# Weights, and the opening's conditioning columns, stored tile by tile in the chip's memory

## The chip, the cores and the metric

The kernel runs on one core of a Trainium2 chip. A core has a matrix engine (TensorE, PE in the profile), a vector engine (VectorE, DVE), a scalar engine (ScalarE, ACT), a general engine (GpSimd, POOL), an engine that here only issues transfers (SyncE, SP), and 16 DMA engines that move data between the memory outside the core (DRAM) and the core's 128-partition scratch memory. The metric is the device time of one execution in microseconds (us). Before the change the median of three runs is 2210.38 us (2209.37 to 2212.17).

## What is computed

A two-layer decoder trunk on 256 tokens of width 2048, all in float32. Layer 0 mixes tokens with a forgetting attention (FoX), layer 1 with a sliding-window attention (SWA); each is followed by a gated feed-forward block with a short convolution. Every sub-layer is shifted, scaled and gated by columns that come from one conditioning vector `c`:

```python
c_act = jax.nn.silu(c)
for i in range(DEPTH):
    mod = c_act @ ada_w[i] + ada_b[i]                    # 2048 x 12288 weights per layer
    sh1, sc1, g1, sh2, sc2, g2 = jnp.split(mod[:, None, :], 6, axis=-1)
    h = x * (1.0 + sc1) + sh1
    y = fox_attention(h, ...) if i % 2 == 0 else swa_attention(h, ...)
    x = layer_norm(ALPHA * x + (1.0 + g1) * y, ...)
    h = x * (1.0 + sc2) + sh2
    y = conv_ffn(h, ...)
    x = layer_norm(ALPHA * x + (1.0 + g2) * y, ...)
```

The weights are most of what is moved: `fox_w_in` 2048 x 6160, `fox_w_o` 2048 x 2048, `swa_w_in` 2048 x 2560, `swa_w_o` 2048 x 2048, and per layer `ffn_w_up` 2048 x 11264, `ffn_w_down` 5632 x 2048 and `ada_w` 2048 x 12288. `ffn` weights and `ada_w` exist once for each layer.

## The kernel before

**The weight stream.** Every matrix product goes through `stream`. It brings a weight tile `w` of 128 partitions x 2 x 512 float32 (512 KB): 256 rows of the weight and 512 of its columns. Partition p holds row p of the first 128 rows and row p of the second 128 rows, so it is filled by two pieces of 2 KB. ACT rounds the tile to the matrix engine's fast format (`wh`, L273), DVE forms the remainder (`wl`, L284), and PE multiplies three times (high by high, high by low, low by high). In `w_mm` the weights are stationary and the 256 tokens stream (banks `ws`, 24 matmuls for a tile), in `x_mm` the tokens are stationary and 512 weight columns stream (banks `xs`, 12 matmuls for a tile).

**The buffers and queues.** The pool `wp` has ten buffers of 512 KB that the tiles `w`, `wo`, `wa`, `wf` and `ln` share. All transfers of weights are issued by SP, in program order; a transfer waits until its buffer is free, and everything behind it waits too. The Tile framework's scheduler sets the order of the instructions on each engine, except where `pin` keeps program order.

**The opening.** Before the first product of layer 0 can be made, the columns `sh1` and `sc1` must be known: 2048 x 4096 numbers of `ada_w`. `opening` makes them in five steps. The first two steps make 256 of the 2048 columns of each of `sh1` and `sc1` (CB = 256), the last three make 512 (CB = 512). A step's tile `wo` has 1024 numbers in each partition: at CB = 256 it holds two row blocks k and k+1, each filled by a transfer of its own (256 KB in pieces of 1 KB), at CB = 512 one row block (512 KB in pieces of 2 KB). DVE multiplies each row block by one column of the activated vector `cact` and adds it into `oacc` (L605 for the first, L607 for the rest); in the first step four of the 16 row blocks go to PE instead. At the end of a step PE sums `oacc` over the partitions by matmuls with a column of ones (`cps`), DVE adds the bias (`cv`, L646), and the step's slice of the input is turned and modulated into `hH` and `hL`. The first products of FoX with those slices (`first_block`) are woven in between, so that weight tiles and `wo` tiles alternate in SP's queue.

**The rest.** The conditioning vectors of the later sub-layers are made in the background: tiles `wa` of `ada_w` (128 x 1024, one piece of 4 KB in each partition, L400) are woven into the weight stream and reduced by DVE (`acc`, L406). `forget` needs the 16 forget-gate columns of `fox_w_in`, which are brought by one transfer `wf` in 2048 pieces of 64 bytes (L825).

Of the kernel before, what the change touches and what calls it, by code (L numbers as in the profile page):

```python
# [17 lines left out]
P = 128  # L18
D = 2048
S = 256  # L20
NT = S // P
KC = D // P
DEPTH = 2
FH = 16
FW = 2048
# [11 lines left out]
WB = 512  # L37
# [4 lines left out]
def hybrid_trunk(ctx: ExitStack, tc: tile.TileContext, a: dict, out: bass.AP):  # L42
    nc = tc.nc
# [12 lines left out]
    def wtile(name="w"):  # L56
        return wp.tile([P, 2, WB], F32, tag="w", name=name)
# [7 lines left out]
    def bank(name="sm"):  # L65
        return psp.tile([P, 512], F32, tag="ps", name=name)
# [7 lines left out]
    def mm(o, lhsT, rhs, start=False, stop=False, **kw):  # L74
        return nc.tensor.matmul(o, lhsT, rhs, start=start, stop=stop, **kw)  # L75

    def pin(ins, on=True):

        if on:
            tc.keep_in_program_order(ins)  # L80
# [38 lines left out]
    x = cst.tile([P, NT, D], F32, name="x")  # L119
# [146 lines left out]
    def stream(wsrc, row0, col, ks, use, spare={}):  # L266

        for kc in ks[::2]:
            r0 = (row0 + kc) * P
            w = wtile()  # L270
            pin(nc.sync.dma_start(w, wsrc[r0:r0 + 2 * P, col:col + WB].rearrange("(k p) f -> p k f", p=P)), False)
            h, l = spare.get(kc) or (hl.tile([P, 2, WB], F32R, tag=n, name=n) for n in ("wh", "wl"))
            pin(nc.scalar.copy(h, w), False)  # L273

            def go(kc=kc, h=h, l=l):
                ahead[0] -= 1
                run_post()
                use(kc, h, l)
                if feeds:
                    feeds.pop(0)()  # L280
                tick()

            def residual_(w=w, h=h, l=l, go=go):
                pin(nc.vector.tensor_tensor(l, w, f32(h), op=ALU.subtract), behind[0] > 0)  # L284
                behind[0] -= 1
                del residuals[go]

            ahead[0] += 1
            weights.add(go)
            residuals[go] = residual_  # L290
            work.append(go)
            settle(2)
# [75 lines left out]
    def tick():  # L368
        ada_tick()
        if not feeds:  # L370
            step()
# [194 lines left out]
    def opening(plan, proj, prep):  # L566


        widths = [1, 1, 2, 2, 2]
        for v in range(2):  # L570
            cols[0, v] = cst.tile([P, KC], F32, tag=f"cv{v}", name="cv")


        onpe = [range(1, KC, 4), ()] + [(KC - 1,)] * 3

        def products(w, c0, CB, kc, ps, first):
            nb = CB // P
            for c in range(2 * nb):
                mm(ps[:, c:c + 1], w[:, c // nb, c % nb * P:(c % nb + 1) * P], cact[:, kc:kc + 1],
                   start=c == 0 and first, stop=kc == KC - 1, skip_group_check=True)  # L580

        def totals(CB, acc, ps, first, last):
            nb = CB // P
            for c in range(2 * nb):
                mm(ps[:, c:c + 1], acc[:, c // nb, c % nb * P:(c % nb + 1) * P], ones[:, 0:1],
                   start=c == 0 and first, stop=last, skip_group_check=True)

        def sums(s_, c0, CB, acc, ps):
            QK = 512 // CB
            pe = onpe[s_]  # L590
            for kq in range(0, KC, QK):
                w = wp.tile([P, QK, 2, CB], F32, tag="w", name="wo")
                for k in range(QK):
                    nc.sync.dma_start(w[:, k], a["ada_w"][0, (kq + k) * P:(kq + k + 1) * P, :2 * D]
                                      .rearrange("p (v f) -> p v f", f=D)[:, :, c0:c0 + CB])
                for k in range(QK):
                    kc = kq + k
                    end = kc == KC - 1
                    if kc in pe:
                        if end:  # L600
                            totals(CB, acc, ps, kc == pe[0], False)
                        products(w[:, k], c0, CB, kc, ps, kc == pe[0] and not end)
                        continue
                    if kc == 0:
                        nc.vector.tensor_scalar_mul(acc, w[:, k], cact[:, kc:kc + 1])  # L605
                    else:
                        nc.vector.scalar_tensor_tensor(acc, w[:, k], cact[:, kc:kc + 1], acc,  # L607
                                                       op0=ALU.mult, op1=ALU.add)
                    if end:
                        totals(CB, acc, ps, not pe, True)  # L610
                yield

        accs = cst.tile([P, D], F32, tag="acc", name="oacc").rearrange("p (c v f) -> p c v f", c=2, v=2)
        pair = 0
        todos = [[(*it, part) for it in items for part in range(3)] for items in plan]
        for s_, todo in enumerate(todos):
            n = len(todo)
            if s_ == len(widths):
                then(lambda: ada.update(rate=1.6))
                for it in todo:  # L620
                    proj(*it)
                break
            CB = widths[s_] * 2 * P
            nb, k0, c0 = CB // P, 2 * pair, pair * 2 * P
            pair += widths[s_]
            acc = accs[:, s_ % 2, :, :CB]
            ps = bank("cps")
            steps = [sums(s_, c0, CB, acc, ps)] * (KC * CB // 512)
            for i, g in enumerate(steps):
                if i == len(steps) // 2:  # L630
                    c = slice(c0, c0 + CB)
                    nc.sync.dma_start(x[:, :, c], a["x"][0][:, c].rearrange("(t p) d -> p t d", p=P))
                if s_ == 1:
                    while todo and n - len(todo) < -(-(i + 1) * n // len(steps)):
                        proj(*todo.pop(0))
                next(g)
                while todo and n - len(todo) < (i + 1) * n // len(steps):
                    proj(*todo.pop(0))

            for _ in range((1, 2, 2, 2, 2)[s_]):  # L640
                proj(*todos[s_ + 1].pop(0))
            for k in range(k0, k0 + nb, 2):
                tps = mod_turn(k, 2 if k == 0 else 1)
                if k == k0:
                    for v in range(2):
                        nc.vector.scalar_tensor_tensor(cols[0, v][:, k:k + nb], ps[:, nb * v:nb * (v + 1)], float(v),  # L646
                                                       acol[:, 0, v * KC + k:v * KC + k + nb],
                                                       op0=ALU.add, op1=ALU.add)
# [159 lines left out]
    def fox(l, j):  # L808
        w_in, w_o = a["fox_w_in"][j], a["fox_w_o"][j]
# [10 lines left out]
        def prep():  # L820
            for b in range(4):
                nc.sync.dma_start(bfc[32 * b:32 * b + FH, :], a["fox_b_f"][j:j + 1].rearrange("l h -> h l"))

            wf = wp.tile([P, KC, FH], F32, tag="w", name="wf")
            nc.sync.dma_start(wf, w_in[:, 3 * FW:3 * FW + FH].rearrange("(k p) f -> p k f", p=P))  # L825
            for q in range(4):
                src = wf[:, q * 4:(q + 1) * 4, :].rearrange("p k (o f) -> p k o f", o=1).broadcast_to([P, 4, 4, FH])
                th, tl = (i[q].rearrange("p k (b f) -> p k b f", b=4)[:, :, :, :FH] for i in (fh, fl))
                split(th, tl, src)
# [144 lines left out]
        for blk, rate in zip((0, 2, 1, 3), (1.6, 1.6, 1.5, 1.4)):  # L974
            then(lambda rate=rate: ada.update(rate=rate))
            q, k, V = [], [], []
            n = done.get((blk, 0), 0)
# [8 lines left out]
            o = old.get(blk, [None] * 3)  # L986
# [219 lines left out]
    for t in range(NT):  # L1206
        mu, rs, _ = moments[t]
        for d in range(D // 512):
            c = slice(d * 512, (d + 1) * 512)
# [2 lines left out]
            nc.sync.dma_start(ov[:, t, c], x[:, t, c])  # L1212


_INS = ["x", "c", "positions", "fox_w_in", "fox_b_f", "fox_w_o", "swa_w_in", "swa_sinks", "swa_w_o",
        "ada_w", "ada_b", "ffn_w_up", "ffn_conv_w", "ffn_conv_b", "ffn_w_down",
        "ln_mix_g", "ln_mix_b", "ln_ffn_g", "ln_ffn_b"]


# [19 lines left out]
```

## Time and profile before

| what | value |
|---|---|
| median of three runs | 2210.38 us (2209.37 to 2212.17) |
| span of the profiled execution, first to last instruction | 2210.7 us |
| PE busy | 2161.9 us (98%) |
| DVE busy | 1811.1 us (82%) |
| ACT busy | 1138.6 us (52%) |
| DMA: moved, mean rate | 602.98 MB, 273 GB/s |
| DMA packets | 274246, of which 243,592 of 2 KB up to 8 KB |

The profiled execution has no other time of its own than its span, which lies inside the range of the three runs. Busy time is the union of an engine's instructions. A matmul's end is modelled, so a PE that is busy throughout can still run below its best pace: the number of matmuls in a stretch tells that, and so does the granted clock (PEclk). "DMA share" is the mean busy share of the 16 DMA engines; it can exceed 1 a little, because the packets of an engine overlap. Times within the execution are counted from the span's start.

### The profile page before, as it was taken

What the parts mean: (1) busy time and instruction counts of PE and PEld (TensorE: products, weight loads), DVE (VectorE), ACT (ScalarE), POOL (GpSimd) and SP (SyncE); (2) the same over time, 40 slices, a digit from 0 to 9 for tenths busy, and PEclk for the clock granted to TensorE, in tenths of its full rate; (3) what the DMA queues carried; (4) which work ended last, traced back from release to release, by engine and by line L of the source; (5) the groups of instructions that cost most, each with busy time, mean ns of one, the idle gap of its engine ahead of it and who ended that gap; (6) DMA issues with size and microseconds to landing.
All of it is one profiled execution on the core that took longest, in us unless ns stands there. A gap on an engine that the chain in (4) does not pass through costs nothing.

```text
span 2210.7 us, 38191 instructions
## 1 busy us (share of the span) xinstructions
PE 2161.9 (98%) x14883; PEld 1973.9 (89%) x14883; DVE 1811.1 (82%) x2487; ACT 1138.6 (52%) x1713; POOL 19.9 (1%) x49
## 2 busy tenths in 40 slices
PE   6999999999999999999999999999999999999997
PEld 5999888789999988999987877789999988999986
DVE  6879998989978989889989888899888655666765
ACT  3435656465555533555534587545555533555541
POOL 0000000000000000000000000000000000000000
PEclk9999999999999999999999999999999999999999
DMA  9999998979978989889988666778888566666663
GB/s 341 367 343 373 347 357 297 329 256 325 344 238 297 323 299 365 287 266 325 311 281 312 229 200 201 258 269 293 281 270 267 188 194 193 195 195 192 195 198 112
DMA packets 274246, 602.98 MB, mean 273 GB/s; under 512 B 21062, under 2 KB 29960, under 8 KB 273552
## 3 DMA queue, kind: packets, MB, share of 16 engines
q1 hardware_dynamic: 273008, 595.85, 80.0%
q0 software_dynamic: 1056, 4.69, 0.6%
q8 instruction: 116, 1.90, 0.4%
q14 instruction: 66, 0.54, 0.1%
HBM read 598.37 MB, written 2.10 MB: 272 GB/s over the span
## 4 chain that ended last, share of the span: by engine, by line
PE 83%; DVE 9%; issue 3%; DMA 2%; ACT 2%; SPq 0%; POOL 0%; DVEq 0%; ACTq 0%; POOLq 0%
PE ws L75 47%; PE xs L75 32%; DVE acc L406 3%; DVE wl L284 2%; DMA wo<-in_ada_w_dram 2%; ACT wh L273 1%; PE sm L527 1%; PE cps L75 1%; PE S L75 1%; DVE pr L736 1%; PE o L75 0%; PE sm L75 0%; PE T L767 0%; DVE oacc L607 0%; DVE x L708 0%
## 5 line engine op out<-in xcount | busy, mean ns | idle before, releaser
L273 ACT CAST wh<-w 128x1024 fp32r<-128x1024 f32 x724 | 761.2, 1053 | 795.9 <-PE ws L75 297.9
L75 PE MATMUL ws<-hH,wh 128*128 128x256 f32 x6656 | 1150.6, 277 | 4.6 <-ACT hH L84 2.1
L284 DVE TENSOR_TENSOR wl<-w,wh 128x1024 fp32r<-128x1024 f32 x724 | 881.6, 1220 | 297.2 <-ACT wh L273 282.1
L75 PEld LDWEIGHTS ws<-hH,wh 128*128 128x128 f32 x6656 | 1011.0, 189 | 8.8 <-ACT hH L84 2.3
L75 PE MATMUL ws<-hH,wl 128*128 128x256 f32 x3328 | 918.3, 277 | 4.5 <-DVE wl L284 4.4
L75 PEld LDWEIGHTS ws<-hH,wl 128*128 128x128 f32 x3328 | 627.7, 189 | 6.3 <-DVE wl L284 6.1
L75 PE MATMUL xs<-wh,gT 128*128 128x512 f32 x1376 | 425.4, 389 | 0.0
L75 PEld LDWEIGHTS xs<-wh,gT 128*128 128x128 f32 x1376 | 258.3, 188 | 53.6
L75 PE MATMUL xs<-wl,gT 128*128 128x512 f32 x688 | 267.8, 389 | 0.0
L75 PE MATMUL xs<-wh,hH 128*128 128x512 f32 x704 | 235.9, 402 | 0.0
L406 DVE SCALAR_TENSOR_TENSOR acc<-wa,cact,acc 128x1024 f32<-128x1024 f32 x180 | 227.8, 1276 | 0.5 <-DMA wa<-in_ada_w_dram 0.5
L406 DVE SCALAR_TENSOR_TENSOR acc<-wa,cactp,acc 128x1024 f32<-128x1024 f32 x128 | 162.1, 1275 | 0.7 <-DMA acc<-in_ada_b_dram 0.7
L75 PEld LDWEIGHTS xs<-wh,hH 128*128 128x128 f32 x704 | 131.5, 189 | 28.9 <-ACT hH L84 0.3
L75 PEld LDWEIGHTS xs<-wl,gT 128*128 128x128 f32 x688 | 129.2, 188 | 26.5
L75 PE MATMUL xs<-wl,hH 128*128 128x512 f32 x352 | 139.4, 397 | 2.5 <-DVE wl L284 2.5
L1123 ACT ACTIVATE u<-ws,ccol 128x256 f32<-128x256 f32 x176 | 96.7, 561 | 62.2 <-PE ws L75 45.2
L75 PE MATMUL xs<-wh,oT 128*128 128x512 f32 x384 | 125.6, 396 | 0.0
L1124 DVE SCALAR_TENSOR_TENSOR u<-ws,ccol,u 128x255 f32<-128x255 f32 x176 | 82.3, 476 | 13.7 <-ACT u L1123 13.3
L75 PEld LDWEIGHTS xs<-wh,oT 128*128 128x128 f32 x384 | 72.1, 188 | 15.0
L1126 DVE SCALAR_TENSOR_TENSOR u<-ws,ccol,u 128x254 f32<-128x254 f32 x176 | 82.9, 476 | 2.0
L75 PEld LDWEIGHTS xs<-wl,hH 128*128 128x128 f32 x352 | 66.6, 189 | 17.7 <-DVE wl L284 4.3
L607 DVE SCALAR_TENSOR_TENSOR oacc<-wo,cact,oacc 128x1024 f32<-128x1024 f32 (+1 forms) x68 | 73.3, 1078 | 6.8 <-DMA wo<-in_ada_w_dram 5.7
(231 smaller groups left out, 1296.8 us busy)
## 6 DMA issues: line engine op xcount, KB each, us to landing
w<-in_ffn_w_up_dram SPq DMA_DIRECT2D x352, 512.0 KB, 4.7
wa<-in_ada_w_dram SPq DMA_DIRECT2D x320, 512.0 KB, 5.6
w<-in_ffn_w_down_dram SPq DMA_DIRECT2D x176, 512.0 KB, 5.0
w<-in_fox_w_in_dram SPq DMA_DIRECT2D x96, 512.0 KB, 7.3
wo<-in_ada_w_dram SPq DMA_DIRECT2D x48, 512.0 KB, 8.9
w<-in_swa_w_in_dram SPq DMA_DIRECT2D x40, 512.0 KB, 4.9
w<-in_fox_w_o_dram SPq DMA_DIRECT2D x32, 512.0 KB, 6.0
w<-in_swa_w_o_dram SPq DMA_DIRECT2D x32, 512.0 KB, 5.5
```

The costliest lines, as they stand in the source:

```text
L75: return nc.tensor.matmul(o, lhsT, rhs, start=start, stop=stop, **kw)
L273: pin(nc.scalar.copy(h, w), False)
L284: pin(nc.vector.tensor_tensor(l, w, f32(h), op=ALU.subtract), behind[0] > 0)
L406: pin(nc.vector.scalar_tensor_tensor(ac, wo, (cactp if row else cact)[:, k:k + 1], ac, op0=ALU.mult, op1=ALU.add), True)
L527: nc.tensor.transpose(o[:, t * P:(t + 1) * P], x[:, t, (k + j) * P:(k + j + 1) * P], ident)
L607: nc.vector.scalar_tensor_tensor(acc, w[:, k], cact[:, kc:kc + 1], acc, op0=ALU.mult, op1=ALU.add)
L736: nc.vector.tensor_tensor_reduce(pr[:, b:e].rearrange("p (a k) -> p a k", k=P), S_ps[:, b:e].rearrange("p (a k) -> p a k", k=P), mk, -1.0, ...
L1123: nc.scalar.activation(u, pf, AF.Identity, bias=cw(CW, f), scale=cw(2, f))
L1124: nc.vector.scalar_tensor_tensor(u[:, 1:], pf[:, :S - 1], cw(1, f), u[:, 1:], op0=ALU.mult, op1=ALU.add)
L1126: nc.vector.scalar_tensor_tensor(u[:, 2:], pf[:, :S - 2], cw(0, f), u[:, 2:], op0=ALU.mult, op1=ALU.add)
```

## The change

On the host, before the launch, the weights are stored in another order: for each tile the 2 KB pieces of a partition lie side by side, and the partitions of a tile follow each other, so that a tile is one run of 512 KB and each partition is filled by one run of 4 KB. This holds for all tiles of `stream`. The opening's slice of `ada_w` is stored once more (`ada_open`) in the same manner, so that a tile of CB = 256 comes in one transfer in place of two. The forget-gate columns become an array of their own (`fox_w_f`), one run of 1 KB for each partition. What lies in the scratch memory after a transfer is the same as before; no instruction of PE, DVE, ACT or POOL is added or removed.

```diff
     def stream(wsrc, row0, col, ks, use, spare={}):
         for kc in ks[::2]:
-            r0 = (row0 + kc) * P
             w = wtile()
-            pin(nc.sync.dma_start(w, wsrc[r0:r0 + 2 * P, col:col + WB].rearrange("(k p) f -> p k f", p=P)), False)
+            pin(nc.sync.dma_start(w, wsrc[(row0 + kc) // 2, col // WB]), False)
...
     def opening(plan, proj, prep):
-        widths = [1, 1, 2, 2, 2]
+        widths = list(STEPS)
...
                 w = wp.tile([P, QK, 2, CB], F32, tag="w", name="wo")
-                for k in range(QK):
-                    nc.sync.dma_start(w[:, k], a["ada_w"][0, (kq + k) * P:(kq + k + 1) * P, :2 * D]
-                                      .rearrange("p (v f) -> p v f", f=D)[:, :, c0:c0 + CB])
+                o = a["ada_open"][(c0 * KC + kq * CB) // 512]
+                nc.sync.dma_start(w.rearrange("p a b c -> p (a b c)"), o)
...
             wf = wp.tile([P, KC, FH], F32, tag="w", name="wf")
-            nc.sync.dma_start(wf, w_in[:, 3 * FW:3 * FW + FH].rearrange("(k p) f -> p k f", p=P))
+            nc.sync.dma_start(wf, a["fox_w_f"][j])
...
+STEPS = (1, 1, 2, 2, 2)
+
+def blocks(w):
+    l, k, n = w.shape
+    return w.reshape(l, k // (2 * P), 2, P, n // WB, WB).transpose(0, 1, 4, 3, 2, 5)
+
+def laid_out(a):
+    out = dict(a)
+    w = a["fox_w_in"]
+    out["fox_w_in"] = blocks(w[:, :, :3 * FW])
+    out["fox_w_f"] = w[:, :, 3 * FW:].reshape(-1, KC, P, FH).transpose(0, 2, 1, 3)
+    for n in ("fox_w_o", "swa_w_in", "swa_w_o", "ffn_w_up", "ffn_w_down"):
+        out[n] = blocks(a[n])
+    steps, c0 = [], 0
+    for s in STEPS:
+        cb = s * 2 * P
+        w = a["ada_w"][0, :, :2 * D].reshape(KC * cb // 512, 512 // cb, P, 2, D)[..., c0:c0 + cb]
+        steps.append(w.transpose(0, 2, 1, 3, 4).reshape(-1, P, 1024))
+        c0 += cb
+    out["ada_open"] = np.concatenate(steps)
+    return out
```

The scheduler is given transfers of another shape, so its order could have moved. SP's queue at the start of the program, before (`wo` are the opening's tiles, `w` the first FoX weights, `x` slices of the input):

```order
L96 DMA rows_76<-in_ada_b_dram 96x128
L594 DMA wo<-in_ada_w_dram 128x2x256 x8
L632 DMA x<-in_x_dram 128x2x256
L594 DMA wo<-in_ada_w_dram 128x2x256 x8
L271 DMA w<-in_fox_w_in_dram 128x2x512 x2
L594 DMA wo<-in_ada_w_dram 128x2x256 x2
L271 DMA w<-in_fox_w_in_dram 128x2x512
L594 DMA wo<-in_ada_w_dram 128x2x256 x4
```

And the same place with the change:

```order
L96 DMA rows_76<-in_ada_b_dram 96x128
L593 DMA wo<-in_ada_open_dram 128x1024 x4
L630 DMA x<-in_x_dram 128x2x256
L593 DMA wo<-in_ada_open_dram 128x1024 x4
L270 DMA w<-in_fox_w_in_dram 128x1024 x2
L593 DMA wo<-in_ada_open_dram 128x1024
L270 DMA w<-in_fox_w_in_dram 128x1024
L593 DMA wo<-in_ada_open_dram 128x1024 x2
```

Two transfers have become one in each tile of the first two steps, 16 fewer in all; the order of the tiles is the same, here and in the rest of SP's queue.

DVE at the end of the opening's second step, before (`wl` are remainders of FoX weights, `oacc` the products, `cv` the step's columns):

```order
L284 TENSOR_TENSOR wl<-w,wh 128x1024
L607 SCALAR_TENSOR_TENSOR oacc<-wo,cact,oacc 128x2x256 x4
L284 TENSOR_TENSOR wl<-w,wh 128x1024
L607 SCALAR_TENSOR_TENSOR oacc<-wo,cact,oacc 128x2x256 x3
L646 SCALAR_TENSOR_TENSOR cv<-cps,acol 128x2 x2
```

And with the change:

```order
L283 TENSOR_TENSOR wl<-w,wh 128x1024
L605 SCALAR_TENSOR_TENSOR oacc<-wo,cact,oacc 128x2x256 x4
L283 TENSOR_TENSOR wl<-w,wh 128x1024
L605 SCALAR_TENSOR_TENSOR oacc<-wo,cact,oacc 128x2x256 x4
L644 SCALAR_TENSOR_TENSOR cv<-cps,acol 128x2 x2
```

One product has moved behind the last remainder: the products of the last two tiles now stand together. Elsewhere on DVE three more instructions change places with a neighbour, on ACT two and on PE seven.

More of the change, by code (lines that the diff above doesn't have):

```diff
@@ L1212, in hybrid_trunk @@
             nc.sync.dma_start(ov[:, t, c], x[:, t, c])
-_INS = ["x", "c", "positions", "fox_w_in", "fox_b_f", "fox_w_o", "swa_w_in", "swa_sinks", "swa_w_o",
-        "ada_w", "ada_b", "ffn_w_up", "ffn_conv_w", "ffn_conv_b", "ffn_w_down",
-        "ln_mix_g", "ln_mix_b", "ln_ffn_g", "ln_ffn_b"]
+STEPS = (1, 1, 2, 2, 2)
[17 more added lines that the diff above has]
+    return out
 def kernel(**inputs):
@@ L1228 @@
     arrays, args = {}, {}
-    for name in _INS:
-        v = _np.ascontiguousarray(inputs[name])
+    for name, v in laid_out({n: _np.asarray(v) for n, v in inputs.items()}).items():
+        v = _np.ascontiguousarray(v)
         arrays[f"in_{name}_dram"] = v
```

## The prediction

> **What bounds the kernel now.** I read the page first, then the stretches of the span, then the chain of waits of the opening, then DVE in order of time, and last the rates of the transfers. From the page:
>
> ```profile
> span 2210.7 us, 38191 instructions
> PE 2161.9 (98%) x14883; PEld 1973.9 (89%) x14883; DVE 1811.1 (82%) x2487; ACT 1138.6 (52%) x1713; POOL 19.9 (1%) x49
> ...
> PE 83%; DVE 9%; issue 3%; DMA 2%; ACT 2%; SPq 0%; POOL 0%; DVEq 0%; ACTq 0%; POOLq 0%
> ...
> w<-in_ffn_w_up_dram SPq DMA_DIRECT2D x352, 512.0 KB, 4.7
> ```
>
> PE is busy for all but 48.8 us, and transfers hold 2% (some 44 us) of the chain that ended last. A change of transfers can win only from those. Where they lie, the stretches say (columns: stretch, length, busy time of PE, weight load, DVE, ACT, POOL with counts, granted clock, DMA share, GB/s):
>
> ```profile
> 0.00:10.00 10.00, 2.52 (x10) 2.14 (x10) 4.37 (x10) 5.75 (x10) 4.10 (x21) 1.00 0.66 199
> 10.00:20.00 10.00, 7.14 (x30) 6.49 (x31) 6.38 (x11) 0.00 (x0) 0.00 (x0) 1.00 1.08 366
> 20.00:30.00 10.00, 8.43 (x43) 8.05 (x44) 8.43 (x14) 5.45 (x7) 0.00 (x0) 1.00 1.08 366
> 30.00:40.00 10.00, 7.24 (x51) 6.46 (x49) 8.93 (x11) 4.65 (x8) 0.00 (x0) 1.00 1.08 364
> 40.00:50.00 10.00, 7.30 (x35) 7.24 (x36) 7.83 (x11) 2.09 (x2) 0.00 (x0) 0.66 1.04 385
> 60.00:150.00 90.00, 90.00 (x623) 84.80 (x622) 75.17 (x72) 36.66 (x45) 2.52 (x5) 0.92 1.01 360
> 150.00:300.00 150.00, 146.08 (x1115) 137.23 (x1114) 137.68 (x197) 87.33 (x168) 5.88 (x12) 1.00 1.01 357
> 500.00:750.00 250.00, 249.33 (x2161) 247.66 (x2161) 226.33 (x291) 138.86 (x190) 0.00 (x0) 1.00 0.89 303
> 1500.00:1750.00 250.00, 250.00 (x2161) 248.20 (x2161) 210.13 (x283) 141.84 (x195) 0.00 (x0) 1.00 0.81 266
> 1750.00:2100.00 350.00, 350.00 (x2506) 327.24 (x2505) 212.80 (x266) 170.06 (x210) 0.00 (x0) 1.00 0.65 194
> ```
>
> From 500 us on PE has no gap and the DMA engines have spare time: a faster transfer there buys nothing. DMA is full from 10 to 300 us, but from 60 to 150 PE is full too, and from 150 to 300 DVE is (137.68 of 150). Only the first 43 us are short of data. The chain there, in order of time (start, length, what):
>
> ```profile
> 11.24 5.89 DMA wo<-in_ada_w_dram
> ...
> 17.21 7.75 DMA wo<-in_ada_w_dram
> ...
> 32.09 7.74 DMA wo<-in_ada_w_dram
> ...
> 40.24 0.75 DVE oacc L607
> ...
> 42.70 1.84 PE cps L75 x8
> 44.54 5.09 PE ws L75 x24
> ...
> 143.14 9.47 DMA wo<-in_ada_w_dram
> ...
> 153.93 2.60 PE xs L75 x10
> ...
> 411.36 3.83 DMA wa<-in_ada_w_dram
> ...
> 417.13 4.74 DMA w<-in_fox_w_o_dram
> ```
>
> The opening's tiles pace it to 40 us, then the sums (`cps`) and PE. Later a transfer is on the chain three times. But the chain names one of two causes that end nearly together; DVE in the opening's second step (24.3 to 42.6 us) shows the other, first as groups of that stretch, then at the ends of steps one and two:
>
> ```profile
> L607 DVE SCALAR_TENSOR_TENSOR oacc<-wo,cact,oacc 128x512 f32<-128x512 f32 x15 | 11.3, 750 | 1.2 <-DMA wo<-in_ada_w_dram 0.9
> L284 DVE TENSOR_TENSOR wl<-w,wh 128x1024 fp32r<-128x1024 f32 x5 | 6.1, 1219 | 0.0
> ```
>
> ```profile
> 17.98 1.54 DVE L607 SCALAR_TENSOR_TENSOR oacc<-wo,cact,oacc 128x512 f32<-128x512 f32 x2 [0.68 <-DMA wo<-in_ada_w_dram]
> 21.48 0.23 DVE L646 SCALAR_TENSOR_TENSOR cv<-cps,acol 128x2 f32<-128x2 f32 x2 [1.96 <-PE cps L75]
> ...
> 38.43 0.75 DVE L607 SCALAR_TENSOR_TENSOR oacc<-wo,cact,oacc 128x512 f32<-128x512 f32 x1 [0.92 <-DMA wo<-in_ada_w_dram]
> ...
> 40.24 2.32 DVE L607 SCALAR_TENSOR_TENSOR oacc<-wo,cact,oacc 128x512 f32<-128x512 f32 x3
> ```
>
> In step two DVE waits for a transfer 0.92 us and is busy otherwise. So step one, to 19.5 us, is paced by transfers, and step two by DVE almost as much.
>
> **What a packet size is worth.** Three stretches, each of mostly one size, as moved at a full DMA: 10 to 16 us (1 KB), 44 to 60 (2 KB), 174 to 178 (4 KB: 1.65 MB in some 404 packets that are not small).
>
> ```profile
> DMA packets 2251, 2.17 MB, mean 362 GB/s; under 512 B 132, under 2 KB 2251, under 8 KB 2251
> ...
> DMA packets 3232, 6.23 MB, mean 390 GB/s; under 512 B 191, under 2 KB 191, under 8 KB 3231
> ...
> DMA packets 453, 1.65 MB, mean 413 GB/s; under 512 B 48, under 2 KB 48, under 8 KB 452
> ```
>
> So a byte in 4 KB pieces takes 362/413 = 0.877 of its time in 1 KB pieces, and 390/413 = 0.944 of that in 2 KB pieces. The Trainium skill ("DMA: Bandwidth & Descriptors", Why small descriptors are slow) gives a smaller loss: about 3 cycles for each packet beside one for 32 bytes. By that, 1 KB to 4 KB would save 6.4% (131 cycles against four times 35) and 2 KB to 4 KB 2.2%. The rows show 12.3% and 5.6%, about twice as much, and with the page's figures the sum below would end near -2.2 us; it goes by the rows.
>
> **The change part by part.** *Step one of the opening.* Its 16 row blocks are 16 x 256 KB = 4.19 MB: 11.6 us at 362 GB/s, 10.15 at 413, so -1.4. Against it stands the tile in one transfer: the last two row blocks now land together, and one product more (0.75 us) follows the last landing: +0.75. The start is the unknown. The first 10 us move only 199 GB/s. If that is the price of many small transfers, all 4.46 MB (with the slice of x) would land from 2.1 us on at 413, by 12.9, and step one end near 14.4 in place of 19.5: -5.1. If the start's slowness has another cause and the single transfer waits for its slowest DMA engine, nothing is left: 0. I take -1.2: the -0.65 from the rates and 0.5 for half as many transfers at the start, nearer to the rates since the rows with a full DMA carry them.
>
> *Step two.* Up to its last row block the DMA brings 4.19 MB of `wo` and six `w` (3.15 MB): -1.4 and -0.45, together with step one -3.2, less 0.75 for the coarser landing. But DVE has 17.4 us of products and remainders there that no transfer shortens; it can give back its 0.92 us at most. The smaller gain decides: -0.9, bounds 0 and -0.9. The one product that moves behind the last remainder costs nothing, since DVE works through both without a gap.
>
> *Steps three to five and the first FoX products.* The 48 tiles of 512 KB and the `w` go from 2 KB to 4 KB. PE is full from 60 to 150 us and the chain runs through PE from 42.7 to 130: 0. The `wo` transfer at 143 us (9.47 us) would take 5.6% less: -0.5, bounds 0 and -1.3.
>
> *`wf`.* Its 2048 pieces of 64 bytes hold up the DMA between 160 and 164 us:
>
> ```profile
> DMA packets 2481, 0.68 MB, mean 171 GB/s; under 512 B 2211, under 2 KB 2211, under 8 KB 2481
> ```
>
> Four us at 360 would have moved 1.44 MB, so about 2 us of DMA time are lost. PE has work queued (its idle time from 150 to 300 us is 3.9 in all), the tile itself is not needed until after 187 us. I take -0.3, bounds 0 and -1.6.
>
> *The rest.* The FoX output weight on the chain at 417 us: 5.6% of 4.74, taken as -0.2, bounds 0 and -1. FFN and SWA weights: 0; the work that hides them is PE's own, 250.00 of 250 us. Were PE 10% faster there, 303 GB/s of demand would come near the DMA's limit, and then 5.6% would count. SP issues 16 transfers fewer; it waits for buffers, not for itself.
>
> Sum: -1.2 - 0.9 - 0.5 - 0.3 - 0.2 = -3.1. Against the profile's own 2210.7 us that is 2207.6; the median of the runs lies 0.3 lower, so 2207.3.
>
> **Rivals.** *The transfers pace more than DVE and PE let me see.* From 60 to 150 us the DMA is at 1.01 of its time, and ACT waits for FoX weights there:
>
> ```profile
> ACT wh L273 <- DMA w<-in_fox_w_in_dram: 36.4, 17, 5.3
> ```
>
> If these waits reach PE, 107 us (43 to 150) shrink by 5.6%, -6.0, on top of -2.5 at 43 us: about 2202. Against it: PE is busy 90.00 of 90.
>
> *The clock.* From 40 to 50 us the granted clock is 0.66: nearly 7 us at half. PE then does 24 `ws` matmuls in 5.09 us. If shorter waits keep the clock up, 3.4 us more are won: 2203.9. It can as well lose the same elsewhere. The Trainium skill ("TensorE: Matmul & The Clock Gate", Part 1) says that the clock halves after an idle window of about 3.4 us, which runs free of the kernel; 0.66 over 10 us, two such windows at half, agrees, and by that rule a shift of the work alone can add or remove one.
>
> *Nothing comes of it.* The runs of 4 KB may go out as 2 KB packets, or the start stays as slow as it is and the coarser tiles take back the rest: 2209.5 to 2211.
>
> *Slower.* A tile in one run of 512 KB puts all 16 engines side by side in one part of the memory. If they hinder each other, the rate falls. The lowest for a busy engine here is 194/0.65 = 298 GB/s (1750 to 2100 us): the 12.06 MB to the end of step two (4.46 + 4.19 + 3.15 and a second slice of x) would take 7.4 us more than at 365, with the coarser landing some 8: 2218. It decides once the rate stays under 340 GB/s, the 303/0.89 of the feed-forward block. Against it: every row of `wa` already is 4 KB, and they go at 413.
>
> **How the numbers follow.** Forecast 0.43, own range 2205 to 2209.5; transfers pace more 0.24; clock 0.12; nothing 0.13; slower 0.08. The range of 2201.5 to 2211.5 holds the first four but for their tails. About 0.2% (4.4 us) is what a measurement of this kernel tells from no change. Faster than 2206: 0.24 + 0.12 and a little of the forecast, 0.38. Within: 0.40 of the forecast and 0.13, 0.53. Slower: 0.09.
>
> **What would show it.** Right: `wo` and `w` packets of 4 KB and over 400 GB/s from 10 to 40 us; the first `cv` near 20.3 us in place of 21.5; the first `ws` after the second step near 42.4 in place of 44.5, with DVE without a gap before it; stretches from 500 us on as before. Wrong: `cv` before 18 us (the start was a matter of transfers), a second step shorter by over 1 us (DVE was not its bound), PE from 60 to 150 us with more matmuls than 623 (the DMA paced it), or a full DMA under 390 GB/s.

## The result and the profile after

The change is faster by about 0.2%: 2204.98 us (median of 12 runs, 2203.63 to 2208.23) against 2209.86 us (12 runs, 2208.09 to 2212.57) of the kernel before, a ratio of 0.9978 with a 95% interval of 0.997 to 0.9986. The forecast was 2207.3, and 3.1 us gained; 4.9 were measured. Two later sets of runs of the same change gave 0.9982 (0.9973 to 0.9991) and 0.9982 (0.9974 to 0.9991), that is 3.5 and 4.1 us. The profiled executions stand 8.2 us apart, more than any of the medians; why is the main question below.

Here are lines of the page of the kernel after: span, busy times, DMA packets, and the shares of the chain that ended last.

```profile
span 2202.5 us, 38162 instructions
...
PE 2156.7 (98%) x14883; PEld 1968.9 (89%) x14883; DVE 1810.4 (82%) x2487; ACT 1139.3 (52%) x1713; POOL 19.9 (1%) x49
...
DMA packets 166598, 602.98 MB, mean 274 GB/s; under 512 B 18758, under 2 KB 19592, under 8 KB 165904
...
PE 84%; DVE 10%; issue 3%; ACT 2%; DMA 1%; SPq 0%; POOL 0%; DVEq 0%; ACTq 0%; POOLq 0%
```

The layout took effect: the same 602.98 MB go in 166,598 packets in place of 274,246, and the DMA's share of the chain is 1% in place of 2%. PE is idle for 45.8 us (48.8 before), and is busy 5.2 us less with the same 14,883 matmuls. So 3.0 of the 8.2 us are waits of PE that are gone, and 5.2 are PE's own pace, which the runs below trace to its clock and not to the transfers.

The stretches of the kernel after (columns as in the prediction: stretch, length, PE, weight load, DVE, ACT, POOL, granted clock, DMA share, GB/s):

```profile
10.00:20.00 10.00, 6.71 (x28) 6.06 (x28) 6.29 (x10) 1.04 (x1) 0.00 (x0) 1.00 1.02 408
20.00:30.00 10.00, 8.42 (x47) 8.12 (x47) 9.85 (x16) 6.34 (x9) 0.00 (x0) 1.00 1.03 411
30.00:40.00 10.00, 6.10 (x41) 5.33 (x39) 9.75 (x13) 4.96 (x7) 0.00 (x0) 0.91 1.03 406
40.00:50.00 10.00, 9.32 (x48) 8.49 (x48) 7.11 (x9) 1.46 (x3) 0.00 (x0) 0.75 1.03 410
...
60.00:150.00 90.00, 89.43 (x630) 83.28 (x629) 78.20 (x76) 35.92 (x43) 2.52 (x5) 0.96 0.98 373
...
500.00:750.00 250.00, 249.33 (x2132) 246.52 (x2132) 226.34 (x291) 139.24 (x191) 0.00 (x0) 1.00 0.87 305
...
1750.00:2100.00 350.00, 350.00 (x2505) 327.24 (x2504) 212.36 (x265) 169.78 (x209) 0.00 (x0) 1.00 0.62 194
```

From 10 to 50 us the DMA moves 406 to 411 GB/s where it moved 364 to 385. Behind 500 us its share falls by 0.02 to 0.03 at nearly the same GB/s: the same bytes cost less of its time, and nobody needs that time. From 1750 to 2100 us PE does 2505 matmuls, as it did 2506.

Rows of VectorE in order of time, after (start, duration, and in brackets the idle time ahead and what ended it):

```profile
20.04 0.23 DVE L644 SCALAR_TENSOR_TENSOR cv<-cps,acol 128x2 f32<-128x2 f32 x2 [1.96 <-PE cps L75]
...
42.26 0.23 DVE L644 SCALAR_TENSOR_TENSOR cv<-cps,acol 128x2 f32<-128x2 f32 x2 [2.02 <-PE cps L75]
```

The second `cv` of before:

```profile
44.58 0.23 DVE L646 SCALAR_TENSOR_TENSOR cv<-cps,acol 128x2 f32<-128x2 f32 x2 [2.02 <-PE cps L75]
```

And all that VectorE waited for from 20 to 45 us after the change (total, times, longest):

```profile
DVE cv L644 <- PE cps L75: 4.0, 2, 2.0
```

The first `cv` comes at 20.04 in place of 21.48, the second at 42.26 in place of 44.58. In the second step VectorE now waits for no transfer at all; before it waited 0.92 us for a `wo`. The chain of waits shows the same end of step two (start, length, what):

```profile
42.22 4.22 PE ws L75 x24
```

The first products start at 42.22 in place of 44.54. This is 2.3 us of lead. The medians show 4.9 and the profiles 8.2.

### The profile page after: what moved, and what is told of

Read it like the earlier page. It is cut to its first block, busy times and chain, and to the rows that moved or that the text cites. A ratio compares the mean times of both kernels' runs of the same rounds, so it can differ in the third digit from the quotient of the medians.

```text
span 2202.5 us, 38162 instructions
## 1 busy us (share of the span) xinstructions
PE 2156.7 (98%) x14883; PEld 1968.9 (89%) x14883; DVE 1810.4 (82%) x2487; ACT 1139.3 (52%) x1713; POOL 19.9 (1%) x49
## 2 busy tenths in 40 slices
DMA packets 166598, 602.98 MB, mean 274 GB/s; under 512 B 18758, under 2 KB 19592, under 8 KB 165904
## 4 chain that ended last, share of the span: by engine, by line
PE 84%; DVE 10%; issue 3%; ACT 2%; DMA 1%; SPq 0%; POOL 0%; DVEq 0%; ACTq 0%; POOLq 0%
PE ws L75 47%; PE xs L75 33%; DVE wl L283 3%; DVE acc L405 3%; DMA wo<-in_ada_open_dram 1%; ACT wh L272 1%; PE cps L75 1%; PE sm L526 1%; PE S L75 1%; DMA w<-in_fox_w_in_dram 1%; PE o L75 1%; DVE pr L734 1%; DVE oacc L605 0%; PE sm L75 0%; PE T L765 0%
## 5 line engine op out<-in xcount | busy, mean ns | idle before, releaser
L75 PE MATMUL xs<-wl,oT 128*128 128x512 f32 x192 | 75.4, 393 | 3.1 <-DVE wl L283 3.1
```

## The experiments

The theory under test was the one of the prediction: the opening's two steps give the gain, and weights in larger pieces give nothing, since PE or VectorE bound the rest. Its rivals were that transfers pace PE up to 150 us, and that the clock decides. Each run is stated against runs of the kernel before on the same chip. "Ratio" is the time over that of before, with its 95% interval in brackets. Code cuts are shortened; `...` marks what is left out.

**The opening alone.** All streamed weights and `wf` stay as before; only `ada_open` is laid out, one transfer for each tile.

```diff
-            nc.sync.dma_start(wf, a["fox_w_f"][j])
+            nc.sync.dma_start(wf, w_in[:, 3 * FW:3 * FW + FH].rearrange("(k p) f -> p k f", p=P))
...
-    out["fox_w_in"] = blocks(w[:, :, :3 * FW])
...
-    for n in ("fox_w_o", "swa_w_in", "swa_w_o", "ffn_w_up", "ffn_w_down"):
+    for n in ():
         out[n] = blocks(a[n])
```

> Only the opening's tiles are stored tile by tile and come in one transfer each; all other weights and the forget-gate columns lie and come as before. Theory (the gain is made in the first two steps of the opening, by their own tiles, and what is more than 2.3 us of it is the clock): the first columns near 20.1 us (before 21.5, with the whole change 20.0), the first matmuls after step two between 42.2 and 42.9 (44.5 and 42.2), and the time 2.5 to 5 us below before. Rival (the FoX weights pace PE from 43 to 150 us): less than 2 us below before, since these weights come as before.

Measured: 2204.94 us (2203.39 to 2211.09), ratio 0.9987 (0.9978 to 0.9997), profiled span 2202.6. VectorE's rows and one stretch of this kernel:

```profile
20.20 0.23 DVE L648 SCALAR_TENSOR_TENSOR cv<-cps,acol 128x2 f32<-128x2 f32 x2 [1.96 <-PE cps L75]
...
42.41 0.23 DVE L648 SCALAR_TENSOR_TENSOR cv<-cps,acol 128x2 f32<-128x2 f32 x2 [2.02 <-PE cps L75]
...
60.00:150.00 90.00, 89.43 (x630) 83.22 (x629) 78.21 (x76) 36.11 (x44) 2.52 (x5) 0.96 1.01 371
```

With the old weights, and the DMA full again (1.01 in place of 0.98), PE does the same 630 matmuls from 60 to 150 us as with the new ones, and its span is that of the whole change to 0.1 us. The transfers of weights don't pace PE there. The ratio is a little nearer to 1 than those of the whole change, with overlapping intervals. Its interval, 0.7 to 4.9 us of gain, would by itself allow the rival's less than 2; it is the count of matmuls that speaks against the rival.

**The streamed weights alone**, with the opening as before.

```diff
-                o = a["ada_open"][(c0 * KC + kq * CB) // 512]
-                nc.sync.dma_start(w.rearrange("p a b c -> p (a b c)"), o)
+                for k in range(QK):
+                    nc.sync.dma_start(w[:, k], a["ada_w"][0, (kq + k) * P:(kq + k + 1) * P, :2 * D]
+                                      .rearrange("p (v f) -> p v f", f=D)[:, :, c0:c0 + CB])
...
```

> Only the streamed weights and the forget-gate columns are stored tile by tile; the opening's tiles lie and come as before. Theory: the first columns at 21.5 us as before, the matmuls after step two at most 0.5 us earlier than 44.5, and the time within 1.5 us of before (PE and DVE hide these transfers). Rival (FoX weights pace): 3 us or more below before, won between 43 and 150 us.

Measured: 2207.86 us (2205.16 to 2211.89), ratio 0.9998 (0.9989 to 1.0006), profiled span 2205.5.

```profile
21.82 0.22 DVE L649 SCALAR_TENSOR_TENSOR cv<-cps,acol 128x2 f32<-128x2 f32 x2 [1.96 <-PE cps L75]
...
44.02 0.23 DVE L649 SCALAR_TENSOR_TENSOR cv<-cps,acol 128x2 f32<-128x2 f32 x2 [2.02 <-PE cps L75]
```

All 728 streamed tiles are laid out here, and nothing comes of it that can be measured; the interval leaves room for up to 2.4 us. The first step is as late as before. The second takes 22.20 us from `cv` to `cv`, the same as in the whole change (22.22): without a wait for a transfer this is VectorE's own work, and the 2.0 us that it waits for PE's sums.

**The late weights alone** (`fox_w_o`, SWA and FFN, 632 of 728 tiles). The edit is against the kernel before. Up to 336 us, when the first tile of `fox_w_o` is issued, this program issues the same instructions and the same transfers as that kernel.

```diff
+def laid_out(a):
+    out = dict(a)
...
+    for n in ('fox_w_o', 'swa_w_in', 'swa_w_o', 'ffn_w_up', 'ffn_w_down'):
+        out[n] = blocks(a[n])
+    return out
```

> Only the weights used after the FoX input projection (FoX output, SWA, both feed-forward blocks: 632 of 728 streamed tiles) are stored tile by tile; FoX input weights, forget-gate columns and the opening come as before. Theory: no change, within 0.7 us of before, since PE is full where these tiles come. Rival (faster landing reaches PE at the stage boundaries, or the tiles' one place in memory slows the transfers): 1.5 us or more off before, either way.

Measured: 2212.12 us (2206.49 to 2214.19), ratio 1.0007 (0.9997 to 1.0016): no gain, so the late weights give nothing that can be measured. The median lies 3.1 us above that of before, where 0.7 at most was expected; these runs had a lower granted clock, and the five of them at 0.992 take 2212.75 us in the mean, where before takes 2212.35 (table below). But the profiled execution spans 2206.3 us, 4.4 less than the profiled one of before. What VectorE waited for from 20 to 45 us in it, and the stretch from 50 to 150 us:

```profile
DVE oacc L610 <- DMA wo<-in_ada_w_dram: 0.3, 1, 0.3
...
50.00:150.00 100.00, 96.94 (x689) 88.96 (x689) 87.06 (x83) 41.66 (x51) 2.52 (x5) 0.98 1.05 386
```

The same stretch of the kernel before:

```profile
50.00:150.00 100.00, 97.89 (x661) 91.67 (x660) 81.63 (x79) 39.62 (x49) 2.52 (x5) 0.91 1.02 363
```

Two executions of the same instructions, with the same old layout: 689 matmuls at a granted clock of 0.98, 661 at 0.91. So one profile against one profile says nothing at the size of some microseconds here, unless the clocks agree. The wait of 0.92 us in step two is not fixed either: it is 0.3 here.

**The change once more**, for a second and a third profile.

> The whole change once more, with a second profile. Theory (2.3 us are won by data up to 42 us, the rest of the first comparison is where the half-clock stretches happen to fall): the first columns at 20.0 us and the matmuls after step two within 0.5 us of 42.2 as in the first profile, but half-clock stretches at other places or of other number; the time 2 to 5 us below before; runs with equal mean clock within about 1 us of each other. Rival (all 4.9 us are the transfers'): the same stretches in the same places, and the same lead at each point of the program as in the first profile.

> The whole change a third time, beside the next kernel on one chip. Theory (data to 42 us, then the clock): the first columns at 20.0 to 20.2 us, the second at 42.2 to 42.4, whatever the total; the time 2 to 5 us below before; runs of equal mean clock some 3 us below those of before. Rival: no lead at equal clock.

Measured: 2205.59 us (2202.45 to 2209.58) and 2204.78 us (2202.88 to 2208.23); profiled spans 2207.8 and 2203.8. The second profile is the useful one, since it had the clock of the profile of before. The cores view of before and of the second profile of the change:

```profile
core 0: 2210.7 us, clock 0.992
```

```profile
core 0: 2207.8 us, clock 0.992
```

Four stretches of before, and the same four, 3 us earlier, of the second profile (the granted clock is the third number from the end):

```profile
36.00:51.00 15.00, 9.53 (x50) 9.10 (x50) 11.26 (x14) 4.10 (x5) 0.00 (x0) 0.77 1.05 380
...
76.00:88.00 12.00, 12.00 (x74) 11.70 (x73) 6.30 (x9) 4.46 (x6) 0.00 (x0) 0.72 0.98 344
117.00:130.00 13.00, 13.00 (x79) 12.29 (x78) 5.46 (x9) 4.33 (x5) 0.00 (x0) 0.74 1.04 378
1205.00:1215.00 10.00, 8.17 (x29) 5.24 (x28) 8.81 (x21) 5.53 (x9) 1.54 (x2) 0.83 0.24 88
```

```profile
33.00:48.00 15.00, 9.83 (x57) 9.46 (x56) 12.69 (x17) 5.04 (x6) 0.00 (x0) 0.77 1.03 409
...
73.00:85.00 12.00, 12.00 (x75) 11.83 (x74) 6.26 (x9) 2.28 (x4) 0.00 (x0) 0.72 0.85 308
114.00:127.00 13.00, 13.00 (x80) 12.38 (x79) 5.79 (x9) 4.17 (x5) 0.00 (x0) 0.74 0.98 373
1202.00:1212.00 10.00, 8.16 (x30) 5.15 (x29) 8.81 (x21) 5.65 (x9) 1.54 (x2) 0.83 0.14 55
```

The clock pattern is the same, moved by about 3 us with the work. In the first profile of the change three of these stretches ran faster:

```profile
76.00:88.00 12.00, 12.00 (x80) 11.27 (x80) 9.96 (x13) 4.71 (x7) 0.00 (x0) 0.86 0.89 311
114.00:127.00 13.00, 13.00 (x90) 12.35 (x90) 7.89 (x12) 4.45 (x7) 0.00 (x0) 0.87 0.97 376
1202.00:1212.00 10.00, 9.55 (x47) 7.61 (x48) 10.00 (x19) 6.64 (x12) 0.00 (x0) 1.00 0.27 84
```

By these rows it kept (0.86 - 0.72) x 12 + (0.87 - 0.74) x 13 + (1.00 - 0.83) x 10 = 5.1 us of full clock more than the second profile, which is 5.3 us longer. So with equal clocks the two executions lie 2210.7 - 2207.8 = 2.9 us apart, and 5.3 of the 8.2 us between the first two profiles are the clock. The same instructions of before and of the second profile say where the 2.9 arise:

```profile
122.33 0.23 DVE L646 SCALAR_TENSOR_TENSOR cv<-cps,acol 128x4 f32<-128x4 f32 x2 [5.31 <-PE cps L75]
...
172.64 3.50 DVE L284 TENSOR_TENSOR wl<-w,wh 128x1024 fp32r<-128x1024 f32 x3 [0.20 <-ACT wh L273]
...
180.40 0.69 DVE L887 SCALAR_TENSOR_TENSOR ql<-ws,qh 128x512 fp32r<-128x512 f32 x1
...
206.18 0.22 DVE L189 CAST posf<-posr 2x128 f32<-2x128 int32 x1 [0.49 <-DMA posr<-in_positions_dram]
...
257.74 0.57 POOL L394 DMA_DIRECT2D acc<-in_ada_b_dram  x1 [48.72 <-PE sm L470]
...
1094.47 0.59 POOL L394 DMA_DIRECT2D acc<-in_ada_b_dram  x1 [620.36 <-DVE red L452]
```

```profile
20.07 0.23 DVE L644 SCALAR_TENSOR_TENSOR cv<-cps,acol 128x2 f32<-128x2 f32 x2 [1.96 <-PE cps L75]
...
42.29 0.23 DVE L644 SCALAR_TENSOR_TENSOR cv<-cps,acol 128x2 f32<-128x2 f32 x2 [2.02 <-PE cps L75]
...
119.73 0.23 DVE L644 SCALAR_TENSOR_TENSOR cv<-cps,acol 128x4 f32<-128x4 f32 x2 [5.39 <-PE cps L75]
...
169.67 3.50 DVE L283 TENSOR_TENSOR wl<-w,wh 128x1024 fp32r<-128x1024 f32 x3 [0.23 <-ACT wh L272]
...
177.74 0.69 DVE L885 SCALAR_TENSOR_TENSOR ql<-ws,qh 128x512 fp32r<-128x512 f32 x1 [0.92 <-ACT qh L884]
...
203.31 0.21 DVE L189 CAST posf<-posr 2x128 f32<-2x128 int32 x1 [0.27 <-DMA posr<-in_positions_dram]
...
254.87 0.57 POOL L393 DMA_DIRECT2D acc<-in_ada_b_dram  x1 [48.65 <-PE sm L469]
...
1091.59 0.59 POOL L393 DMA_DIRECT2D acc<-in_ada_b_dram  x1 [620.34 <-DVE red L451]
```

And two pieces of the second profile's chain of waits:

```profile
42.26 4.90 PE ws L75 x24
...
151.28 2.59 PE xs L75 x10
```

The lead of the second profile is 1.41 us at the first `cv`, 2.29 at the second, 2.60 at the third (122.33 against 119.73), 2.65 on PE at 154 (153.93, behind the `wo` at 143 us, against 151.28), 2.97 at 172, 2.66 again at 180, 2.87 at 257 and 2.88 at 1094. Step one and step two give 2.3 of the 2.9. The rest comes in small steps. From 44 to 55 us the 24 matmuls behind the sums take 4.90 us in place of 5.09, which is the half clock ending earlier beside the work (0.2). Then ScalarE no longer rounds a weight tile ahead of `hH`, as it did in its order before (0.2). At 206 us VectorE waits 0.27 us for the transfer of the positions where it waited 0.49 (0.2); in the first profile of the change this wait is 0.48, so it isn't the layout's. So 2.3 us are the layout, 0.2 more come of the moved order, and the rest is what differs from one execution to another. From 257 us on nothing is won.

Many runs show about the same. Here are the means of all runs of before and of the whole change that list their granted clock, grouped by it (four runs of before at 0.991, with a mean of 2213.44 us, have no counterpart):

| granted clock | before, us (runs) | the change, us (runs) | difference |
|---|---|---|---|
| 0.992 | 2212.35 (14) | 2209.58 (1) | -2.8 |
| 0.993 | 2209.56 (19) | 2207.71 (7) | -1.8 |
| 0.994 | 2208.83 (43) | 2205.19 (14) | -3.6 |
| 0.995 | 2207.18 (13) | 2203.81 (10) | -3.4 |
| 0.996 | 2205.70 (1) | 2202.66 (2) | -3.0 |

At equal clock the change wins about 3 us. Over all these runs the means differ by 4.2 (2209.43 in 94 runs, 2205.28 in 34), since the mean clock is higher with the change, 0.99415 against 0.99353: an estimated 0.00062 x 2207 = 1.4 us. Grouped in the same way, the opening alone is 3.2 us below before at 0.995 (6 runs) and 1.6 at 0.992 (3 runs); the streamed weights alone are 0.9 below at 0.994 (5 runs).

**Two transfers for a tile.** The whole change, but each tile of the first two steps comes in two transfers, one for each row block, in pieces of 2 KB.

```diff
-                o = a["ada_open"][(c0 * KC + kq * CB) // 512]
-                nc.sync.dma_start(w.rearrange("p a b c -> p (a b c)"), o)
+                o = a["ada_open"][(c0 * KC + kq * CB) // 512].rearrange("p (a b c) -> p a b c", a=QK, b=2)
+                for k in range(QK):
+                    nc.sync.dma_start(w[:, k], o[:, k])
```

> As the whole change, but a tile of the first two steps comes in two transfers again, one for each row block, in pieces of 2 KB (in place of one transfer in pieces of 4 KB, or before two in pieces of 1 KB). Theory (the piece size counts, and the coarser tile costs one product, 0.75 us, that the rates pay back): pieces of 2 KB at 390 GB/s against 1 KB at 362 give 0.85 us of the 1.4, the finer landing 0.75: the first columns between 19.7 and 20.5 us, the time within 1.5 us of the whole change. Rival (the number of transfers makes the start slow): the first columns at 21 us or later, the time 1.5 us or more above the whole change.

Measured: 2208.05 us (2204.08 to 2210.58), ratio 0.9991 (0.9981 to 1), span 2202.3; the first `cv` at 20.39, the second at 42.60. That is 0.3 us behind the whole change at both places, so the rival (21 us or later) is refuted. Two row blocks that can land one after the other in pieces of 2 KB are no better than both at once in pieces of 4 KB. The median lies 3.1 us above the first one of the whole change, where 1.5 at most was expected; the intervals of the ratios overlap, so the times don't separate the two.

**One transfer in pieces of 1 KB.** The whole change, but the tiles of the first two steps are stored so that their one transfer fills each partition by four runs of 1 KB.

```diff
-                nc.sync.dma_start(w.rearrange("p a b c -> p (a b c)"), o)
+                wv = w.rearrange("p a b c -> p (a b c)")
+                if CB == 256:
+                    o = o.rearrange("p f -> (p f)").rearrange("(q p f) -> p q f", q=4, p=P)
+                    wv = wv.rearrange("p (q f) -> p q f", q=4)
+                nc.sync.dma_start(wv, o)
...
+        if cb == 256:
+            t = t.reshape(-1, P, 4, 256).transpose(0, 2, 1, 3).reshape(-1, P, 1024)
```

> As the whole change, but the tiles of the first two steps, still one transfer each, are filled in four runs of 1 KB for each partition in place of one of 4 KB. Theory (the piece size is what counts): 1 KB pieces at 362 GB/s and the coarser landing, so the first columns between 21.5 and 22.3 us, not before the kernel before (21.5), the time 1 to 3 us above the whole change. Rival (half as many transfers is what counts): the first columns at 20 to 20.7 us as in the whole change.

Measured: 2205.94 us (2203.51 to 2209.14), ratio 0.9984 (0.9975 to 0.9993), span 2204.2.

```profile
21.11 0.23 DVE L652 SCALAR_TENSOR_TENSOR cv<-cps,acol 128x2 f32<-128x2 f32 x2 [1.96 <-PE cps L75]
```

The first `cv` stands between what the two theories gave. Against the whole change, whose first `cv` came at 20.04, 20.07 and 20.14, the size of the pieces alone is worth 1.0 us, by this one execution. Against the old opening, seen at 21.46 (late weights), 21.48 (before), 21.82 (streamed weights) and 22.37 (before with idle matmuls, below), three things that changed together are worth 0.35 to 1.3 us: half as many transfers, the coarser landing, and the place in memory, since the 1 KB pieces of a tile lie in one run here and in rows of `ada_w`, 48 KB apart, before. The run with two transfers has finer landing and smaller pieces as well, so it doesn't separate them, and the place in memory wasn't tested by itself.

**Two row blocks of step two on PE.** If VectorE bounds step two, products taken from it must shorten it.

```diff
-        onpe = [range(1, KC, 4), ()] + [(KC - 1,)] * 3
+        onpe = [range(1, KC, 4), (13, 14)] + [(KC - 1,)] * 3
```

> The whole change, and two of the sixteen row blocks of the opening's second step (the 14th and 15th) are multiplied and summed on PE in place of DVE. Theory (DVE bounds the second step): two products of 0.76 us leave DVE behind the last landing, the second columns come 1.2 to 1.5 us earlier than 42.3 us. Rival (transfers bound it): less than 0.4 us earlier, or later.

> The whole change with two row blocks of the second step on PE, a second time, beside the whole change on one chip. Theory (PE bounds everything behind 42 us, and the clock decides what of a lead lasts): the second columns again near 40 us, the time 0 to 2 us below the whole change. Rival (the lead of 2.2 us at 40 us lasts in full): 2 us or more below the whole change.

Measured in two sets: 2204.49 us (2200.86 to 2206.17), ratio 0.9978 (0.9969 to 0.9987), and 2204.18 us (2199.4 to 2207.32), ratio 0.9977 (0.9968 to 0.9986). The second `cv`, and PE's clock later, in the first of them:

```profile
40.03 0.23 DVE L648 SCALAR_TENSOR_TENSOR cv<-cps,acol 128x2 f32<-128x2 f32 x2 [1.28 <-PE cps L75]
...
113.00:125.00 12.00, 12.00 (x66) 11.21 (x67) 6.66 (x10) 2.39 (x5) 0.00 (x0) 0.72 0.90 345
```

VectorE does bound step two: the second `cv` comes 2.2 us earlier than in the change's first profile, and at 39.67 in the second of the two sets. 1.5 of the 2.2 are two products of 0.76; the other 0.7 is VectorE's wait for PE's sums, 1.28 us in place of 2.02, since these took 0.95 us at full clock in place of 1.83 at half. But the span is 2202.5, that of the change: at 113 to 125 us this execution has a clock of 0.72, where the change's first profile had 0.87 in nearly the same stretch. On PE the lead is still 2.3 us at 110 us, and 12 x 0.15 = 1.8 us of it are gone there. The intervals overlap those of the change (0.9973 to 0.9991), so a gain beyond it isn't shown.

**Holding the clock up.** Matmuls whose result isn't used (ten calls, which stand as twenty in the trace) are put in PE's gap ahead of the sums of step two, in the whole change and, apart from it, in the kernel before.

```diff
+                if s_ == 1 and i == len(steps) - 1:
+                    spin(bank("spin"), 10)
                 next(g)
```

> The whole change, and ten idle matmuls of 384 columns (their result is not used) in PE's gap ahead of the second step's sums, so that PE is not idle there. Theory (an idle PE brings the half clock behind it): the half-clock stretch at 38 to 45 us goes or halves, the matmuls behind the second step gain 1.7 to 3.4 us, and the time is 1 to 3.4 us below the whole change at most runs. Rival (the clock falls regardless of PE's own idle time): stretches as before, the time within 1 us of the whole change or above it.

> The kernel before, with the same ten idle matmuls in the same gap. Theory (clock): 1 to 3.4 us below before, with transfers as before. Rival: no change.

Measured: with the change 2206.14 us (2204.2 to 2206.88), ratio 0.9985 (0.9976 to 0.9993); in the kernel before 2208.84 us (2206.39 to 2210.74), ratio 0.9996 (0.9987 to 1.0005). The idle matmuls and the second `cv` of the first, and two stretches of it:

```profile
35.20 6.61 PE L75 MATMUL spin<-mask,ident 128*128 128x384 f32 x20
...
42.64 0.23 DVE L650 SCALAR_TENSOR_TENSOR cv<-cps,acol 128x2 f32<-128x2 f32 x2 [2.31 <-PE cps L75]
```

```profile
36.00:47.00 11.00, 11.00 (x59) 8.27 (x58) 8.55 (x12) 2.10 (x3) 0.00 (x0) 1.00 1.03 409
...
113.00:125.00 12.00, 12.00 (x67) 11.20 (x66) 5.57 (x9) 2.71 (x4) 0.00 (x0) 0.72 0.99 379
```

The low clock of the first stretch is gone (1.00), but at 113 to 125 us it is 0.72, and no time is won in either kernel. The theory's gain failed to appear in both. The run is not a clean test of it: the idle matmuls outlast the gap. VectorE's last product ends at 40.34 us, the sums start only at 41.81, and the second `cv` comes 0.4 us later than in the whole change (42.64); in the kernel before the sums start at 44.72, 1.0 us behind the last product. It shows one thing about the table above: with the idle matmuls the whole change has a mean clock of 0.9956 in its eleven runs, higher than without, and is no faster. Part of that clock was held up while PE had nothing useful to do, which raises the mean and saves no time. So the mean clock compares runs of one program safely, and runs of two programs only roughly; the two profiles with the same low stretches are the firmer ground for the 2.9 us.

## Why the prediction was right

**The bound, and where the gain lies.** Right. With the opening alone a gain is there that can't be told from the whole change's; with the weights alone there is none that can be measured. The four signs named for being right all came: over 400 GB/s from 10 to 40 us, the first `cv` at 20.04, no wait of VectorE for a transfer in step two and the first `ws` behind it at 42.22, and the stretches from 500 us on as before.

**Step one, -1.2.** Measured -1.4 between the profiles, and -1.3 to -2.3 between all executions with the old and the new opening. The total was close, its parts were not. The larger pieces gave 1.0 us by the run with 1 KB pieces, less than the 1.4 forecast from the rates. The coarser landing, priced at +0.75, did not show: together with half as many transfers and the tile's one place in memory it gained at least 0.35 us, where a loss of 0.25 (+0.75 - 0.5) was forecast. These weren't measured apart. So this term came out near by errors that offset each other, which is luck.

The Trainium skill ("DMA: Bandwidth & Descriptors", Why small descriptors are slow) states a fixed cost of about 3 cycles for each packet; by the 6.4% worked out from it in the prediction the larger pieces would give an estimated 0.74 us of 11.6. The 1.0 measured lies between that and the 1.4 from the rows.

**Step two, -0.9.** Right, in mechanism and size: it gives back VectorE's wait and no more, 23.10 us from `cv` to `cv` before and 22.22 after. It takes 22.1 to 22.2 us wherever VectorE waits for no transfer and has its old work (22.5 with the idle matmuls, which hold up the sums), and two products moved away shorten it. The wait is not the same in each execution: with the old opening and the old FoX weights it is 0.92 before, 1.17 before with idle matmuls and 0.33 with the late weights, 0.8 in the mean. With the old opening and the new FoX weights it is gone too, in the one execution seen; so the six `w` tiles of this step may give it back as well as its `wo`.

**The later `wo` at 143 us, -0.5; `wf`, -0.3; the FoX output weight at 417 us, -0.2.** Mis-sized: they gave nothing. At equal clocks the lead is 2.60 ahead of the `wo` and 2.65 on PE behind it. `wf` does let VectorE's remainders at 172 us come 0.3 sooner, as priced, and they don't come sooner with the opening alone, where `wf` is the old one; but at 180 us this is gone. At 257 and 1094 us the lead is 2.87 and 2.88, so nothing came at 417. The chain of waits passed through these transfers without their being what PE lacked. In their place three steps of 0.2 us arose, two from 44 to 55 us and one at 206, that the prediction didn't have. So of the forecast's 3.1 us steps one and two, 2.1, stand against 2.3 measured, and the other 1.0 was wrong. That the sum lies so near 2.9 is in part luck.

**The rivals.** *Transfers pace more*: refuted, since old weights with a full DMA give PE the same 630 matmuls. The sign named for it, more than 623 matmuls from 60 to 150 us, did appear and misled: a clock of 0.96 in place of 0.92 made it. *Nothing comes of it*: refuted by the ratio, whose interval ends at 0.9986. *Slower*: refuted; whole tiles in one place move 406 to 411 GB/s, far above 340. *The clock*: priced as one outcome apart from the forecast, while it is added to it in every run. At equal clock the forecast's 3.1 us stands against 2.9 measured; the 3.5 to 4.9 us of the medians are that and what the clock added, by the means over all runs an estimated 1.4 us. Whether the change raises the mean clock, because PE waits less in the opening, or the runs fell so, stays open: the attempt to hold the clock up removed one low stretch, but delayed the sums, and won no time.

**Behind 500 us.** As forecast, the stretches stand as before.

## What to carry to other kernels

A layout that makes transfers cheaper wins only where an engine waits for a transfer that is late: here 1.4 us in the first 20 us and the 0.9 us of one wait behind them. The 728 streamed tiles, whose transfers the work hides, gave nothing that could be measured. The chain of waits shows a candidate, and the work of the engine that needs the tile next tells whether it counts. Where a gain of 0.2% is claimed or sought, compare executions with the same granted clock in the same stretches, since one profile against another can differ by 5 us of clock alone. An experiment that fills a gap must be shown in its trace not to outlast the gap.

## What was not expected of the hardware

The granted clock falls in short stretches even where PE is busy throughout (76 to 88 us: 12.00 of 12.00 busy, clock 0.72), and the pattern has variants. Before and the change's second profile show the same values at places 3 us apart; two executions of the one program (the first and second profile of the change) show others from 76 us on. The Trainium skill ("TensorE: Matmul & The Clock Gate", Part 1) calls the activity window free-running and the number of slow matmuls of one kernel variable from run to run; the variants agree with that.

The traces have a hint why the pattern can also move along with the work. Between 70 and 165 us each low stretch begins at most 5 us behind the start of a group `cps`, sums made by matmuls with a single column; this holds in all thirteen profiled executions. In the kernel before the first group starts at 77.90 us, with 32 such matmuls, and the clock is at half from 80 us to 86.8. Not every group is followed so: with the late weights alone and with two transfers for a tile the same group, at 76.8 and 75.6 us, and the next two, from 112 to 119 us, leave the clock at 1.00. That such a group counts as little work for the clock is a guess that no run here tests.

The runs' times follow this clock: before takes 2212.35 us at a mean of 0.992 and 2207.18 at 0.995. And the opening's transfers are not steady: with the same transfers of step one the first `cv` came at 21.46 to 22.37 us in four executions with the old opening, while the new one gave 20.04 to 20.20 in five with the whole change's two steps (20.13 and 19.90 with two row blocks of step two on PE).
